# FoX attention with its decay as a table in memory, MLA attention with key halves side by side and whole second values, both written as ordered lists

## Chip, cores and metric

The kernel runs on one core of a Trainium2 chip. The metric is the device time in microseconds (us) of one execution, as the median of several; lower is better. The core's engines are TensorE (PE, matrix products; PEld is its load of the stationary operand), VectorE (DVE), ScalarE (ACT), GpSimd (POOL) and SyncE (SP, which here issues all DMAs). They run side by side and wait for each other through semaphores.

## The reference, cut to what matters

Two layers on a stream of 256 positions by 1024 features, all in float32. Each layer is a half-step SwiGLU network (1024 to 2 x 2816 and back), an attention mixer, a second half-step network and a gated input embedding, with a LayerNorm after each. The two mixers are what the change touches:

```python
# layer 0: forgetting attention (FoX), 16 heads of 64
cum = cumsum(log_sigmoid(f_logit), axis=1)            # [head, position]
s = q @ k.T / 8 + cum[:, :, None] - cum[:, None, :]   # then the causal mask, softmax, @ v
# layer 1: multi-head latent attention (MLA), 16 heads; keys and values from a shared latent
s = (q_nope @ k_nope.T + q_rope @ k_rope.T) / sqrt(192)   # 128 + 64 wide; then mask, softmax
o = softmax(s) @ v                                        # v: 128 per head
```

Sequence blocks are 128 long. Block 0 of the queries sees keys 0 to 127, block 1 sees keys 0 to 255.

## The kernel before, in words

**Split products.** Nearly every product is made of float32 numbers split in two: a high part rounded to the type float32r and a low part, the remainder. ACT writes the high part and DVE the low one (`parts`, line 497; for weights `split`, line 174). `mm3` (line 482) then issues three products, high x high, high x low and low x high, which add up in one PSUM bank. All 1 MB pieces of weights come over SP into three raw buffers, are split into ten or more slots, and are used in the order of a recording made beforehand. The steps `S.fill`, `S.ahead`, `S.later`, `S.split_now` and `S.pump` decide, when the program is built, where in ACT's and DVE's queues the next weight is split: `ahead` puts the high part now and leaves the low one, `later` puts that low one, `fill n` splits until n weights are ready beyond the one in use.

**FoX** (`fox`, line 858). After the values, a chain of small operations (`gates`, line 938, pieces s1 to s6, taken one at a time between weights) makes the running sum of the gates in a tile of 32 x 256 on ACT, DVE and POOL, and writes -8 x the sum, split in two, into `negc`. Heads go in pairs j = 0 to 7, one head on the PE's upper 64 rows and one on the lower 64. For a pair: keys and queries (`gen_k`, `gen_q`, 2.7 us of PE each), `QK` (line 1017), whose first products put the gates' term into the bank by a stationary column that selects one head (`sel` x `negc`, 384 columns), then `least` (line 1038; adds the causal mask and takes the least scaled value per row), `exps` (ACT), `divide` (reciprocals on DVE, four divisions on POOL), `T` (transposes of the probabilities on PE, then `parts`), `AV` (line 1097). `O` multiplies by the output weights. A loop over pairs of pairs (line 1146) sets the order.

**MLA** (`mla`, line 1272). The order of all steps is a list of strings, `ORDER` (line 47), that a loop at line 1556 carries out. For each head h: `gen` (keys and queries without position), `QK` (line 1449), `sm` (softmax: two DVE minima with the mask, two exponentials), `div`, `T`, `AV` (line 1512) and `O`. A query block's scores are three products of the split halves and two with the rotary keys, each 128 columns wide for block 0 and 256 for block 1. `AV` has, for the first 128 keys, three products of 256 columns, and for the second 128 keys, which only block 1 sees, three products of 128 columns with values split in two (`V` at line 1307 writes the high part, `vlo` at line 1319 the low one).

Of the kernel before, what the change touches and what calls it, by code (L numbers as in the profile page):

```python
# [45 lines left out]
VRING = ((0, 0), (1, 1), (1, 2), (2, 2))  # L46
ORDER = (
# [43 lines left out]
class Recorder:  # L91
# [10 lines left out]
    lend = reclaim = check = load = busy = pair = split = split_pieces = ahead = later = split_now = fill = pump  # L102
# [3 lines left out]
class Stream:  # L106
# [173 lines left out]
    def pair(self, n):  # L280

        self.busy(act=n)
        self.dve_t = max(self.dve_t, self.act_t + 100)
        self.busy(dve=n)
# [113 lines left out]
class Trunk:  # L398
    def __init__(self, nc, pools, a, S, rec):
        self.nc, self.a, self.S = nc, a, S  # L400
        self.sb, self.ps = pools
        self.rec = rec
        self.bg = deque()
        self.setup()
# [92 lines left out]
    def parts(self, hi, lo, src):  # L497

        self.nc.scalar.activation(hi, src, AF.Copy)  # L499
        self.nc.vector.tensor_tensor(lo, src, hi.bitcast(F32), op=ALU.subtract)  # L500
        self.S.pair(cols(src))
# [356 lines left out]
    def fox(self, li):  # L858
# [60 lines left out]
        sel = self.tl([128, 16], F32R, "sel", 1)  # L919
        negc = self.tl([128, 384], F32R, "negc", 1)  # L920
# [6 lines left out]
        nc.gpsimd.memset(negc.bitcast(F32), 0.0)  # L927
        sf = fs[:, 1792:1808]
        nc.gpsimd.tensor_tensor(sf, self.ident[:, 16:32], self.ident[:, 48:64], op=ALU.add)
        nc.gpsimd.tensor_tensor(sf, sf, self.ident[:, 80:96], op=ALU.add)  # L930
        nc.gpsimd.tensor_tensor(sel, sf, self.ident[:, 112:128], op=ALU.add)
# [4 lines left out]
        m8 = fs[fr, 1536:1792]  # L936

        def gates():
# [4 lines left out]
            def s1():  # L943
# [3 lines left out]
                self.S.busy(act=2400)  # L947
# [19 lines left out]
            def s4():  # L967
                nc.scalar.activation(negc[fr, 0:128], m8[:, 0:128], AF.Copy)
                nc.scalar.activation(negc[fr, 128:384], m8, AF.Copy)
# [127 lines left out]
        def AV(j, what=None):  # L1097
# [11 lines left out]
            if what:  # L1109
                what()  # L1110
# [35 lines left out]
        for a in range(0, 6, 2):  # L1146
# [6 lines left out]
            if a:  # L1153
                AV(a - 1)
# [519 lines left out]
```

## Time and profile before

| | |
|---|---|
| median of 3 runs | 1069.97 us (1069.09 to 1071.38) |
| the profiled execution's own time | 1069.07 us |
| its span, first to last instruction | 1067.3 us |
| mean granted TensorE clock | 0.998 |
| FoX attention, first QK to the last output product | from about 224 to 302 us of the span |
| MLA attention, first key generation to the last output product | from about 729 to 855 us |

The profile is one execution on the chip. Engine records of PE overlap, because products are pipelined; a distance from start to start is the pace. A page gives busy time and share of each engine, the chain of work that ended last, groups of instructions by line, and DMA issues. The trace behind it answers by window, by tile, by group and as a timeline. An arrow `a<-b,c` reads "a is written from b and c". Names as `h`, `y`, `tr` are PSUM banks, `P` probabilities, `PT` their transposes, `g` values or gates, `fs` the gates' scratch tile (in MLA the latent and rotary keys), `negc` the gates' term.

### The profile page before, as it was taken

The page shows a single profiled execution, that of the slowest core. Times are in us where ns is not written, and L with a number is a line of the kernel's source. Part 1 is how long each engine was busy: PE and PEld are TensorE (multiplying, and loading weights), DVE is VectorE, ACT ScalarE, POOL GpSimd, SP SyncE. Part 2 cuts the span into 40 slices and gives each one's busy share as a digit, 9 for nine tenths or more (in the row PEclk, how much of TensorE's full clock was granted, in tenths as well). Part 3 has the DMA queues.
Part 4 walks back from the last instruction along what each step waited for, and adds up shares of the span by engine and source line. Part 5 has one row for each costly group of instructions (what it writes and reads, how often), then busy time and mean ns, then how long its engine had stood idle before and what let it go on. Part 6 is the DMA issues. An engine that isn't in the chain of part 4 may idle for free.

```text
span 1067.3 us, 17503 instructions
## 1 busy us (share of the span) xinstructions
PE 1056.7 (99%) x7236; PEld 970.6 (91%) x7236; DVE 718.1 (67%) x1029; ACT 542.6 (51%) x805; POOL 68.1 (6%) x94
## 2 busy tenths in 40 slices
PE   9999999999999999999999999999999999999996
PEld 8989998999889999998899998989999889898986
DVE  6675555878797545458966464578887886454566
ACT  5564442667645434444565454436675466354431
POOL 0000000233200000000330000000000000000000
PEclk9999999999999999999999999999999999999999
DMA  8885643543348655454487555413434568555502
GB/s 299 325 295 215 247 162 119 186 175 121 115 180 301 232 186 192 146 203 139 169 294 259 180 194 187 154 59 123 137 140 158 198 244 308 181 204 182 191 4 79
DMA packets 33091, 199.58 MB, mean 187 GB/s; under 512 B 3698, under 2 KB 5490, under 8 KB 12148
## 3 DMA queue, kind: packets, MB, share of 16 engines
q1 hardware_dynamic: 33012, 198.47, 51.8%
q8 instruction: 57, 0.93, 0.4%
q14 instruction: 22, 0.18, 0.1%
HBM read 197.40 MB, written 1.05 MB: 186 GB/s over the span
## 4 chain that ended last, share of the span: by engine, by line
PE 97%; issue 1%; POOL 0%; DVE 0%; ACT 0%; DMA 0%; SPq 0%; DVEq 0%; ACTq 0%; POOLq 0%
PE y L490 36%; PE h L490 35%; PE tr L490 23%; PE tr L494 2%; DMA raw<-in_w_dram 0%; PE h L494 0%; PE tr L1087 0%; DVE x L575 0%; POOL fs L957 0%; POOL fs L950 0%; ACT hl L194 0%; SPq L360 0%; SPq L476 0%; POOL fs L956 0%; ACT hl L232 0%
## 5 line engine op out<-in xcount | busy, mean ns | idle before, releaser
L195 DVE TENSOR_TENSOR hl<-raw,hl 128x1024 fp32r<-128x1024 f32 (+2 forms) x260 | 305.7, 1194 | 146.7 <-ACT hl L194 146.1
L194 ACT ACTIVATE hl<-raw 128x1024 fp32r<-128x1024 f32 (+2 forms) x260 | 262.9, 1031 | 183.4 <-PE y L490 97.5
L490 PE MATMUL h<-xT,hl 128*128 128x256 f32 x1584 | 187.8, 278 | 1.1 <-DVE hl L234 0.5
L490 PEld LDWEIGHTS h<-xT,hl 128*128 128x128 f32 x1584 | 184.3, 189 | 2.5 <-ACT xT L499 0.9
L490 PE MATMUL y<-hl,g 128*128 128x512 f32 x792 | 185.6, 390 | 0.0
L490 PEld LDWEIGHTS y<-hl,g 128*128 128x128 f32 x792 | 147.5, 188 | 29.8
L490 PE MATMUL tr<-xT,hl 128*128 128x256 f32 x1464 | 170.8, 277 | 0.0
L490 PEld LDWEIGHTS tr<-xT,hl 128*128 128x128 f32 x1464 | 168.6, 188 | 0.5
L490 PE MATMUL h<-hl,xT 128*128 128x512 f32 (+2 forms) x294 | 65.2, 373 | 0.0
L490 PEld LDWEIGHTS h<-hl,xT 128*128 128x128 f32 x294 | 51.9, 188 | 9.7 <-DVE xT L500 0.3
L490 PE MATMUL y<-hl,xT 128*128 128x512 f32 (+3 forms) x330 | 59.7, 331 | 0.0
L490 PEld LDWEIGHTS y<-hl,xT 128*128 128x128 f32 x330 | 50.1, 188 | 5.6 <-ACT xT L499 0.4
L567 POOL TENSOR_TENSOR rs<-ve,mhalf 128x1 f32<-128x1 f32 x16 | 15.1, 943 | 619.3 <-DVE ve L566 619.3
L500 DVE TENSOR_TENSOR g<-P,g 128x512 fp32r<-128x512 f32 x38 | 26.3, 693 | 26.6 <-ACT g L499 26.6
L490 PE MATMUL y<-hl,otb 128*128 128x512 f32 x168 | 42.9, 396 | 0.0
L499 ACT ACTIVATE xT<-tr 128x512 fp32r<-128x512 f32 x28 | 16.2, 597 | 48.8 <-PE tr L494 48.8
L499 ACT ACTIVATE g<-P 128x512 fp32r<-128x512 f32 x38 | 24.0, 632 | 32.7 <-DVE P L684 32.7
L195 DVE TENSOR_TENSOR qk<-raw,qk 128x1024 fp32r<-128x1024 f32 (+2 forms) x23 | 28.0, 1217 | 16.1 <-ACT qk L194 16.1
L195 DVE TENSOR_TENSOR otb<-raw,otb 128x1024 fp32r<-128x1024 f32 (+1 forms) x22 | 26.5, 1206 | 17.7 <-ACT otb L194 17.7
L490 PEld LDWEIGHTS y<-hl,otb 128*128 128x128 f32 x168 | 30.2, 188 | 5.6
L194 ACT ACTIVATE otb<-raw 128x1024 fp32r<-128x1024 f32 (+1 forms) x22 | 22.9, 1039 | 19.4 <-PE y L490 10.8
L194 ACT ACTIVATE qk<-raw 128x1024 fp32r<-128x1024 f32 (+2 forms) x23 | 24.0, 1045 | 16.3 <-PE tr L490 6.6
(264 smaller groups left out, 1431.9 us busy)
## 6 DMA issues: line engine op xcount, KB each, us to landing
raw<-in_ffn_in_dram SPq DMA_DIRECT2D x85, 1024.0 KB, 5.0
raw<-in_ffn_out_dram SPq DMA_DIRECT2D x44, 1024.0 KB, 5.0
raw<-in_pg_dram SPq DMA_DIRECT2D x8, 1024.0 KB, 4.8
raw<-in_mo_dram SPq DMA_DIRECT2D x8, 1024.0 KB, 4.7
raw<-in_kq_dram SPq DMA_DIRECT2D x8, 640.0 KB, 4.1
gb<-in_ln_g_dram SPq DMA_DIRECT2D x8, 512.0 KB, 5.8
gb<-in_ln_b_dram SPq DMA_DIRECT2D x8, 512.0 KB, 7.7
raw<-in_fk_dram SPq DMA_DIRECT2D x4, 1024.0 KB, 4.8
```

Source lines behind the costliest of these rows:

```text
L194: nc.scalar.activation(hi, src, AF.Copy)
L195: nc.vector.tensor_tensor(lo, src, hi.bitcast(F32), op=ALU.subtract)
L490: self.nc.tensor.matmul(out, lhsT, rhs, start=start, stop=stop)
L494: self.nc.tensor.transpose(out, in_, self.ident)
L499: self.nc.scalar.activation(hi, src, AF.Copy)
L500: self.nc.vector.tensor_tensor(lo, src, hi.bitcast(F32), op=ALU.subtract)
L567: nc.gpsimd.tensor_tensor(rs, ve, self.mhalf, op=ALU.pow)
```

## The change

1. **FoX, the gates' term.** The products with `sel` and `negc` are gone, and so are these tiles. The running sum times -8 is stored to DRAM (`fox_c`). For each pair j a table `mb[:, j % 2]` of 128 x 2 x 384 is loaded from there, the same row in all 128 partitions (step `dl j`, two DMAs of 128 and 256 columns per head), and POOL writes the causal mask into it (step `dm j`, two selects). `least` adds this table where it added the mask. The table lies in the space of the LayerNorm's `gb`, which is loaded after the last `least` now (step `gb`). Four steps of the gates' chain go from POOL to DVE, and its pieces come closer together.
2. **MLA, QK.** For query block 0 the products that share a stationary operand are one: the high and low key halves lie side by side as 256 columns, so that five products of 128 columns become 256, 128 and 256. The low sum stands in columns 128 to 255, and DVE adds it to the mask before the minima.
3. **MLA, second values.** The values of the second 128 keys are no longer split: they are kept as whole float32, the transposed probabilities for them as well (`tr`, an ACT copy of 128 columns), and one product replaces three. Four of the `vlo` steps go, and `T` splits 256 columns in place of 384.
4. **Lists.** FoX follows a list `FOX` as MLA follows `ORDER`, and both have finer steps: a split is a high step on ACT and a low step on DVE (`ka kd`, `qa qd`, `ta td`, `ua ud`, `oa od`, `ga gd`), the softmax is `mi` or `le`, `ex`, `rec`, `div`. Both are in a new order. In MLA the divisions of heads 2, 3, 4, 10 and 12 go from DVE to ACT.

```diff
+FOX = (
+    "gk 0", "ka 0", "kd 0", "gq 0", "qa 0", "qd 0", "gk 1", "ka 1", "kd 1", "gq 1", "qa 1", "qd 1", "hold 1",
+    "flush", "gt", "lend 0", "QK 0", "QK 1", "le 0", "ex 0", "a", "dl 2", "gk 2", "le 1", "ka 2", "kd 2",
+    "dl 3", "rec 0", "l", "ex 1", "div 0", "gq 2", "qa 2", "qd 2", "rec 1", "dm 2", "dm 3", "a", "l", "a", "l",
+    "gk 3", "ka 3", "kd 3", "T 0", "ta 0", "td 0", "ua 0", "ud 0", "div 1", "a", "l", "a", "l", "f 3", "f 4",
+    "gq 3", "qa 3", "qd 3", "AV 0", "oa 0", "T 1", "od 0", "ta 1", "td 1", "ua 1", "back", "ud 1", "QK 2",
+    "QK 3", "le 2", "AV 1", "a", "dl 4", "oa 1", "od 1", "ex 2", "le 3", "gk 4", "ka 4", "dl 5", "ex 3",
+    "rec 2", "div 2", "kd 4", "l", "gq 4", "qa 4", "qd 4", "rec 3", "div 3", "dm 5", "a", "dm 4", "l", "a", "l",
...
+    "ua 5", "f 3", "ta 5", "QK 7", "td 5", "ud 5", "f 2", "le 6", "AV 5", "oa 5", "ex 6", "f 1", "le 7", "od 5",
+    "ex 7", "lend 1", "rec 6", "div 6", "rec 7", "div 7", "gb", "O 0 0", "f 2", "O 1 0", "a", "l", "f 3",
+    "O 3 0", "O 4 0", "T 6", "ta 6", "O 2 0", "O 5 0", "td 6", "ua 6", "ud 6", "a", "l", "f 1", "f 3", "AV 6",
...
+        mb = self.tl([128, 2, 2, 384], F32, "gb", 1)
...
+        def decay_load(j):
+
+            if not self.rec:
+                o = mb[:, j % 2]
+                for c0, n in ((0, 128), (128, 256)):
+                    row = self.fox_c[2 * j, 0:1]
+                    src = bass.AP(tensor=row.tensor, offset=row.offset, ap=[[0, 128], [256, 2], [1, n]])
+                    nc.sync.dma_start(o[:, :, c0 : c0 + n], src)
+
+        def decay_mask(j):
+
+            for c0 in (0, 256):
+                o = mb[:, j % 2, :, c0 : c0 + 128]
+                nc.gpsimd.affine_select(
+                    out=o, in_=o, pattern=[[0, 2], [-1, 128]], compare_op=ALU.is_ge, fill=NEG,
+                    base=0, channel_multiplier=1,
+                )
...
             def s5():
...
+                self.dma(self.fox_c, m8[16:32, :])
+                for j in range(2):
+                    decay_load(j)
+                    decay_mask(j)
...
-            self.bg.extend((s1, rest, rest, s2, rest, rest, s3, rest, s4, s5, s6))
+            self.bg.extend((s1, s2, s3, s4, rest, rest, s5))
...
-            for s in range(2):
-                h = 2 * j + s
-                self.mm(
-                    sb[s][:, 0:384], sel[half[s], h : h + 1].to_broadcast([64, 128]), negc[half[s], :],
-                    True, False,
-                )
...
-                        out=sb[s][:, c0:c1], in0=sb[s][:, c0:c1], in1=self.mask[:, c0:c1],
+                        out=sb[s][:, c0:c1], in0=sb[s][:, c0:c1], in1=mb[:, j % 2, s, c0:c1],
...
-            o = v[t, g] = self.tl([128, 2, 512], F32R, "g4", 5)
-            nc.scalar.activation(o[:, 0, :], ps, AF.Copy)
+            if t:
+                o = v[t, g] = self.tl([128, 512], F32, "g4", 5)
+                nc.scalar.activation(o, vps.pop((g, t)), AF.Copy)
...
-            for q0, c0, c1 in ((0, 0, 128), (128, 128, 384)):
-                w = c1 - c0
-                self.mm3(
-                    b[:, c0:c1], lambda i: o[:, i, q0 : q0 + 128],
-                    lambda i: o[:, i, 256 : 256 + w], True, False,
-                )
-                for i in (0, 1 + (h % 2 if h < 8 else 1)):
-                    self.mm(b[:, c0:c1], zT[:, h, q0 : q0 + 128], kr[:, i, 0:w], False, i > 0)
+            r = 1 + (h % 2 if h < 8 else 1)
+            two = b[:, 0:256].rearrange("p (i c) -> p i c", i=2)
+            self.mm(two, o[:, 0, 0:128], o[:, :, 256:384], True, False)
+            self.mm(b[:, 0:128], o[:, 1, 0:128], o[:, 0, 256:384], False, False)
+            self.mm(two, zT[:, h, 0:128], kr[:, 0 : r + 1 : r, 0:128], False, True)
+            self.mm3(
+                b[:, 256:512], lambda i: o[:, i, 128:256], lambda i: o[:, i, 256:512], True, False)
+            for i in (0, r):
+                self.mm(b[:, 256:512], zT[:, h, 128:256], kr[:, i, :], False, i > 0)
...
+            t = P[:, 384:512]
+            nc.vector.tensor_tensor(t, b[:, 128:256], self.mask[:, 0:128], op=ALU.add)
+            seg = ((0, b[:, 0:128], t), (128, b[:, 256:512], self.mask[:, 128:384]))
...
-            self.parts(o[:, 0, :], o[:, 1, :], b[:, 0:384])
-            PT[h] = o
+            raw = self.tl([128, 128], F32, "p1", 1)
+            left["T", h] = o[:, 0, 0:256], o[:, 1, 0:256], b[:, 0:256]
+            left["raw", h] = raw, b[:, 256:384]
+            PT[h] = o, raw
...
-            for m, (i, jj) in enumerate(((0, 0), (0, 1), (1, 0))):
-                self.mm(
-                    ps[:, 128:256], v[1, g][:, i, c : c + 128], o[:, jj, 256:384], False, m == 2
-                )
+            self.mm(ps[:, 128:256], v[1, g][:, c : c + 128], raw, False, True)
```

More of the change, by code (lines that the diff above doesn't have):

```diff
@@ L100, in pump @@
         pass
-    lend = reclaim = check = load = busy = pair = split = split_pieces = ahead = later = split_now = fill = pump
+    lend = reclaim = check = load = busy = pair = follow = split = split_pieces = ahead = later = split_now = fill = pump
     between, hl, hold = {}, {}, False
@@ L282, in pair, with follow @@
         self.busy(act=n)
+        self.follow(n)
+    def follow(self, n):
         self.dve_t = max(self.dve_t, self.act_t + 100)
@@ L497, in parts, with high, low @@
     def parts(self, hi, lo, src):
+        self.high(hi, src)
+        self.low(hi, lo, src)
+    def high(self, hi, src):
         self.nc.scalar.activation(hi, src, AF.Copy)
+        self.S.busy(act=cols(src))
+    def low(self, hi, lo, src):
         self.nc.vector.tensor_tensor(lo, src, hi.bitcast(F32), op=ALU.subtract)
-        self.S.pair(cols(src))
+        self.S.follow(cols(src))
     def transposed(self, t, src, halves=(0, 1), ring="tr"):
@@ L918, in fox @@
         bf = self.tl([128, 1], F32, "bf", 1)
-        sel = self.tl([128, 16], F32R, "sel", 1)
-        negc = self.tl([128, 384], F32R, "negc", 1)
+        self.tl([128, 16], F32, "gap2", 1)
+        mb = self.tl([128, 2, 2, 384], F32, "gb", 1)
         cq = self.tl([128, 16, 2], F32, "cq", 1)
@@ L999, in fox, with high, g, low @@
         VA(1)
-        st, PT = {}, {}
+        st, PT, left = {}, {}, {}
         qk = self.own([128, 2, 2, 512], F32R, "qk")
+        def high(f):
+            def g(j):
+                for hi, _, src in left[f, j] if isinstance(left[f, j], list) else [left[f, j]]:
+                    self.high(hi, src)
+            return g
+        def low(f):
+            def g(j):
+                x = left.pop((f, j))
+                for y in x if isinstance(x, list) else [x]:
+                    self.low(*y)
+            return g
         OT = []
@@ L1008, in gen @@
             o = qk[:, j % 2]
-            self.parts(o[:, 0, c0 : c0 + 256], o[:, 1, c0 : c0 + 256], ps[:, 0:256])
+            left[key, j] = o[:, 0, c0 : c0 + 256], o[:, 1, c0 : c0 + 256], ps[:, 0:256]
         def gen_k(j):
@@ L1425, in zT_last, with high, g, low @@
             S.busy(act=512)
-        st, PT = {}, {}
+        st, PT, left = {}, {}, {}
+        def high(f):
+            def g(h):
+                hi, _, src = left[f, h]
+                self.high(hi, src)
+            return g
+        def low(f):
+            return lambda h: self.low(*left.pop((f, h)))
+        def raw_copy(h):
+            self.high(*left.pop(("raw", h)))
         def gen(h):
@@ L1446, in gen @@
             o = home["qk"][:, h % 2]
-            self.parts(o[:, 0, :], o[:, 1, :], ps)
+            left["gen", h] = o[:, 0, :], o[:, 1, :], ps
         def QK(h):
@@ L1550, in mla @@
             dq=dq, rms=rms, dqs=dq_scale, cqT=cq_transpose, V=V, vlo=vlo, qr=q_rope, rope=rope, rc=rope_copy, rot=rotate, zT=zT_first,
-            zs=z_split, zU=zT_last, gen=gen, QK=QK, sm=softmax, div=divide, T=T, AV=AV, O=O, y=room, hold=hold,
+            zs=z_split, zU=zT_last, gen=gen, QK=QK, mi=minima, ex=exps, rec=recip, div=divide, T=T, AV=AV,
+            ga=high("gen"), gd=low("gen"), ta=high("T"), tr=raw_copy, td=low("T"), oa=high("AV"), od=low("AV"), O=O, y=room, hold=hold,
             f=S.fill, a=S.ahead, l=S.later, XT=lambda t, n: self.XT(t, (n,)),
```

176 lines of the change are left out of this document (57 added, 119 removed), and 69 rows, old and new, of tables (FOX, ORDER).

## The prediction, made before the changed kernel ran

> **What bounds the kernel now.** I read the page first, then the chain of waits, the busy times by window, and the timeline of the two attention stages. A row has its start and its length in us, then engine, line, operation, out<-in, shape and count.
>
> ```profile
> span 1067.3 us, 17503 instructions
> ...
> PE 1056.7 (99%) x7236; PEld 970.6 (91%) x7236; DVE 718.1 (67%) x1029; ACT 542.6 (51%) x805; POOL 68.1 (6%) x94
> ...
> PE 97%; issue 1%; POOL 0%; DVE 0%; ACT 0%; DMA 0%; SPq 0%; DVEq 0%; ACTq 0%; POOLq 0%
> ```
>
> TensorE (PE) is busy for 99% of the span and is 97% of the chain that ended last. Records overlap in the pipeline, so a duration there is no price; prices are the distances from start to start. A piece of the chain gives one, and the windows (length, then busy us of PE, PEld, DVE, ACT, POOL, granted clock, DMA share, GB/s) give the room beside it:
>
> ```profile
> 28.35 10.88 PE h L490 x96
> ```
> ```profile
> 224.00:242.00 18.00, 18.00 (x174) 17.36 (x174) 14.14 (x41) 11.15 (x31) 6.05 (x8) 1.00 0.57 212
> 735.00:760.00 25.00, 25.00 (x179) 23.15 (x179) 21.58 (x53) 16.11 (x39) 0.00 (x0) 1.00 0.30 98
> ```
>
> A 256-column product costs 10.88/96 = 113 ns. In both stages that change PE never idles at full clock, and VectorE (DVE), the next one, is 79% (14.14/18) and 86% (21.58/25) busy. So PE work that goes is worth its price, as long as nothing else comes late.
>
> **MLA, on PE.** One head's AV, then the next head's QK, then key generation:
>
> ```profile
> 745.83 0.80 PE L490 MATMUL h<-PT,g 128*128 128x256 f32 x6
> 746.47 0.50 PE L490 MATMUL tr<-qk 128*128 128x128 f32 x3
> 746.80 0.39 PE L490 MATMUL tr<-fs,xT 128*128 128x128 f32 x2
> 747.03 0.57 PE L490 MATMUL tr<-qk 128*128 128x256 f32 x3
> 747.44 0.40 PE L490 MATMUL tr<-fs,xT 128*128 128x256 f32 x2
> 747.67 0.85 PE L490 MATMUL h<-fs,hl 128*128 128x256 f32 x6
> ```
>
> QK takes 747.67 - 746.47 = 1.20 us: five 128-column products in 0.56 (112 ns each, as much as 256 columns cost) and five 256-column ones in 0.64. Side by side, the five narrow ones become 256, 128 and 256. Eight products are then 8 x 113 = 0.90 to 8 x 128 = 1.02 us (0.64/5 = 128 holds the extra 0.07 at the change of width). That saves 0.18 to 0.30; I take 0.28, nearest to the 113 row, since only one change of width is left.
>
> AV takes 0.64: three 256-column products (0.34) and three 128-column ones (0.30). These three become one product of whole fp32 values. The trace has one such product, the 384-column warm-up:
>
> ```profile
> 2.00 0.85 PE L466 MATMUL y<-mask 128*128 128x384 f32 x1
> 2.65 1.06 PE L494 MATMUL tr<-ident 128*128 128x128 f32 x4
> ```
> ```profile
> 750.76 0.49 PE L494 MATMUL tr<-ident,P 128*128 128x128 f32 x3
> ```
>
> One call leaves two records; this is the second, 0.65 us to the next start, so 0.217 per 128 columns. PE is then at about half pace: four transposes take 1.06, while later three take 0.49 (some 0.6 for four). Warm, a pass should cost 0.108 and the product, two passes, 0.217. AV saves 0.30 - 0.217 = 0.08, at most 3 x 0.112 - 0.217 = 0.12; at the early pace it loses 0.30 - 0.433 = -0.13. I take 0.09. Per head 0.37, in 16 heads **5.9 us** (0.05 to 0.42 per head: 0.8 to 6.7).
>
> **FoX, on PE.** The third QK block, two pairs of heads on 64-row halves that run together:
>
> ```profile
> 239.03 0.38 PE L494 MATMUL tr<-ident,P 128*128 128x128 f32 x2
> 239.34 0.44 PE L490 MATMUL y<-negc,sel 64*128 64x384 f32 x2
> 239.62 0.86 PE L490 MATMUL y<-qk 64*128 64x128 f32 x12
> 240.31 0.33 PE L490 MATMUL y<-negc,sel 64*128 64x384 f32 x2
> 240.48 0.85 PE L490 MATMUL y<-qk 64*128 64x128 f32 x12
> 241.26 0.97 PE L490 MATMUL h<-PT,g 128*128 128x512 f32 x3
> ```
>
> The gate products (negc) cost 240.48 - 240.31 = 0.17 inside a block and 0.28 at its entry, where 0.11 is start-up that the first qk pair may inherit. All go: 4 x (0.17 + 0.17) = **1.4 us** in four blocks, 0.9 if the entry's goes over to the next pair nearly whole, 1.8 if nothing does.
>
> **Beside PE, MLA.** Group rows (count | busy us, mean ns):
>
> ```profile
> L500 DVE TENSOR_TENSOR PT<-tr,PT 128x384 fp32r<-128x384 f32 x16 | 8.8, 549 | 0.7 <-ACT PT L499 0.7
> L500 DVE TENSOR_TENSOR otb<-h,otb 128x256 fp32r<-128x256 f32 x10 | 4.2, 416 | 0.5 <-ACT otb L499 0.5
> L1470 DVE CUSTOM_DVE_ANT_0 tr<-tr,mask 128x128 f32<-128x128 f32 x16 | 4.7, 292 | 0.0
> ```
>
> DVE gains 16 adds of 128 columns (some 0.29 each, 4.7 us) and loses 16 x (0.549 - 0.416) = 2.1 in the remainders of P and four value remainders of 512 columns, at least 0.55 each, 2.2: nothing on balance, since five divisions leave it as well. ScalarE (ACT), 64% busy (16.11/25), takes these five and 16 short copies of whole P. PE's products hide all of it, so I cost it at nothing; where a head's chain outlasts that cover, it is rival A. **The order**: PE's list in MLA is the old one but for seven swaps of neighbours, and in FoX but for the output products, so no product is moved to a place where its operands are much younger, with one exception below; what moves is where ACT and DVE do their pieces. That costs nothing by itself and can lose or win only at waits, of which the windows show none.
>
> **Beside PE, FoX.** The table's way is new: POOL writes m8, a store, broadcast loads, POOL masks, then the minima.
>
> ```profile
> 217.64 0.41 POOL L964 TENSOR_SCALAR fs<-fs 32x256 f32<-32x256 f32 x1 [1.08 <-DVE fs L963]
> ```
> ```profile
> 225.09 0.30 DVE L1044 CUSTOM_DVE_ANT_0 y<-y,mask 128x128 f32<-128x128 f32 x1 [0.33 <-PE y L490]
> ```
> ```profile
> out_dram<-x SPq DMA_DIRECT2D x3, 256.0 KB, 2.0
> g<-in_p_dram SPq DMA_DIRECT2D x4, 128.0 KB, 4.9
> gb<-in_ln_b_dram SPq DMA_DIRECT2D x8, 512.0 KB, 7.7
> ```
> ```profile
> L455 POOL TENSOR_SCALAR_AFFINE_SELECT mask<-mask 128x128 f32<-128x128 f32 x2 | 0.5, 295 | 1.2 <-PE y L466 1.2
> ```
>
> m8 ended at 218.05; four POOL steps go to DVE, so I take 216. Store 2.0, loads 0.8 to issue and 4.9 to land, two selects of 256 columns 0.6 to 1.2 (one to two times 295 ns each): 224.3 to 224.9, just before the minima's 225.09. With no gain, and store and loads at 7.7 each: 218.05 + 15.4 + 1.2 = 234.7, 9.6 late. I take 0 and keep that end. T 0 gives 0.8 of it back (next rows). Two waits are added on SP, for m8 and for the store to land, and each later load waits for the minima two pairs before; behind them on SP stand weight loads alone, which have three raw buffers and ten split slots ahead, so that is free. In all 16 loads of 3.1 MB (8 x 128 x 768 x 4 bytes) join a DMA share of 0.57. On DVE four steps of some 0.41 (L964's shape) come in and three conversions go; weight splits queue behind them, under the same ten slots.
>
> ```profile
> 230.92 2.43 POOL L1076 TENSOR_SCALAR P<-P,su 128x128 f32<-128x128 f32 x4 [12.88 <-DVE su L1072]
> ```
> ```profile
> 234.15 0.60 PE L1087 MATMUL tr<-ident,P 128*128 128x128 f32 x4
> ```
> ```profile
> 228.94 0.16 DVE L1051 TENSOR_TENSOR tt<-tt,cq 128x4 f32<-128x4 f32 x1
> ```
> ```profile
> 232.87 4.11 POOL L1076 TENSOR_SCALAR P<-P,su 128x256 f32<-128x256 f32 x5
> 238.59 0.60 PE L1087 MATMUL tr<-ident,P 128*128 128x128 f32 x4
> ```
>
> T 0 follows its divisions (end 233.35) by 0.8, T 1 (ends 236.98) by 1.6. The new list puts masks 2 and 3 ahead of division 1 on POOL, and mask 3 waits for loads that follow minima 1 (229.1): + 0.4 + 4.9 = 234.4, its selects to 235.6, four divisions of 2.43 to 3.6 us (232.87 + 4.11 - 233.35) to 238.0 to 239.2, against T 1 at about 238.2. Bounds 0 and, with a landing of 7.7, 3.8; I take **0.6 us lost**. Later tables load a pair ahead of their use and mask after the divisions. The exception is T 6: one output product less stands before it.
>
> ```profile
> 280.25 1.63 POOL L1076 TENSOR_SCALAR P<-P,su 128x128 f32<-128x128 f32 x4 [10.22 <-DVE su L1072]
> ```
> ```profile
> 282.87 0.60 PE L1087 MATMUL tr<-ident,P 128*128 128x128 f32 x4
> ```
> ```profile
> 297.76 0.74 DVE L575 SCALAR_TENSOR_TENSOR x<-x,mv,gb 128x512 f32<-128x512 f32 x1
> ```
>
> Its divisions end at 281.88, 1.0 ahead. Six products of 512 columns less (12 x 113 = 1.36) and the block's 0.34 less bring T 6 to 281.2; the list puts minima 7 ahead of AV 5's remainders on DVE, so that the divisions end between 280.5 and 282.3: 0 to 1.1 lost, I take 0. The LayerNorm's gb now loads after minima 7, which end before 280.25: + 0.8 + 7.7 = 288.8, well before 297.76: free.
>
> **Sum.** 5.9 + 1.4 - 0.6 = 6.7 us. The profiled execution took 1069.07 (span 1067.3 and 1.8 around it): 1062.4. The median of the runs shown, 1069.97, is 0.9 above it, so I forecast **1063.3**.
>
> **Rivals.** (A) MLA is bound by a head's chain, not by PE. QK to T gets 0.29 longer, T to AV 0.13 shorter, and PE gives 0.37 less cover. For: DVE is 86% busy. Against: the window shows no PE idle time, and other products lie between. All lost: 1063.3 + 5.9 = 1069.2; half: 1066.2. (B) The whole-value product costs four 128-column slots: 4 x 0.112 = 0.45 against 0.30 (the early pace gives 0.433), so AV loses 0.13 instead of gaining 0.09: 16 x 0.22 = 3.5, 1066.8. For: fp32 has no warm row. Against: the warm-up left two records, not four. The Trainium skill, "FP8 and Floating Point Precision", section "TensorE Precision Notes", speaks against the change: true FP32 takes four passes through the array, where the split takes three. By it, at this kernel's price of a narrow product, the time is B's; the trace agrees only as far as the two records each run at two columns' time per column. (C) Slower: the table's store and loads queue behind weight loads. Place: T 0; price 9.6 - 0.8 = 8.8, so 1063.3 + 8.8 = 1072.1; it turns the gain into a loss once minima 0 starts after about 233. For: 212 GB/s in that window, and one late landing holds everything behind it on SP. Against: a DMA share of 0.57, and three landings in a row at the worst row. (D) Stalls go with the finer order or the bounds fall low: under 1060.7.
>
> **How the numbers follow.** Forecast 0.62 (1060.7 to 1065.5), A 0.17, B 0.08, C 0.07, D 0.06. The low end is the sum with 6.7, 1.8, no lost 0.6 (1061.5) and 0.8 for stalls removed; the high end, 1067.5, takes in B and half of A. A measurement of this kernel tells 0.2% from no change (1067.8 and 1072.1). Faster: 0.62 + 0.06 + 0.08 + 0.11 of A = 0.87; same: 0.06 of A + 0.02 of C = 0.08; slower 0.05.
>
> **What would show it.** MLA QK from 1.20 to about 0.92 and AV from 0.64 to 0.55, start to start; two fp32 records of about 108 ns per AV (B: over 200); no negc rows, FoX blocks of 1.92 at about 1.58. PE idle before T (A) or before T 0 and T 1 (C, the lost 0.6). I am wrong if PE's idle time in the two stages grows by more than 2 us.

## The result, and the profile after

The changed kernel takes **1067.79 us** (median of 14 runs, 1065.49 to 1068.79), the kernel before, run beside it, 1070.15 (14 runs, 1068.83 to 1072.72): a ratio of 0.9975, 95% interval 0.9966 to 0.9983. It is faster by 2.4 us where 6.7 were forecast, and lies just above the range given (1060.7 to 1067.5).

Two profiles are compared by the starts of products that both kernels have. The **FoX stretch** runs from the first QK product of FoX to the first output product of the FFN behind it, the **MLA stretch** from key generation 0 to the first output product of the last FFN. "Changed, again" is a later run of the same kernel (e14). A "remainder" below is the low half that DVE writes from a PSUM bank; the bank is free for the next product when it is done. Numbers behind T, QK, AV and "division" are those of the pair in FoX and of the head in MLA.

| stretch (us) | before | changed | changed, again |
|---|---|---|---|
| start to first output product of FFN 1 | 60.83 | 63.43 | 61.02 |
| that FFN, up to its last output product | 126.96 | 126.94 | 126.96 |
| from there to FoX's first QK | 36.14 | 35.54 | 35.92 |
| FoX | 134.66 | 135.85 | 135.91 |
| FFN, per-layer embedding, FFN, MLA's start | 370.03 | 370.03 | 370.04 |
| MLA | 174.17 | 170.62 | 170.72 |
| last FFN and end | 164.50 | 164.58 | 164.58 |
| span | 1067.3 | 1067.0 | 1065.2 |

MLA gains 3.55 (5.9 forecast), FoX loses 1.19 (a gain of 0.8 forecast), the stretch ahead of it gains 0.2 to 0.6. The first stage, 2.6 longer in the first pair of profiles, is no part of the change (run e14). The busy times on the page of the changed kernel:

```profile
span 1067.0 us, 17478 instructions
...
PE 1053.0 (99%) x7172; PEld 965.5 (90%) x7172; DVE 716.0 (67%) x1032; ACT 545.7 (51%) x829; POOL 69.5 (7%) x100
```

The windows of the two stretches in the kernel before and then in the changed one (length, then busy us of PE, PEld, DVE, ACT, POOL, granted clock, DMA share, GB/s):

```profile
223.93:358.59 134.66, 134.62 (x997) 123.80 (x997) 106.77 (x211) 81.94 (x168) 24.36 (x34) 1.00 0.52 190
...
728.62:902.79 174.17, 174.13 (x1196) 159.66 (x1195) 143.71 (x277) 107.04 (x204) 1.84 (x2) 1.00 0.51 183
```
```profile
225.91:361.75 135.84, 134.23 (x981) 122.33 (x981) 108.58 (x213) 83.42 (x170) 33.02 (x48) 1.00 0.61 214
...
731.78:902.40 170.62, 169.71 (x1148) 154.60 (x1147) 141.81 (x280) 111.54 (x230) 1.85 (x2) 1.00 0.53 187
```

PE was never idle in either stretch before (0.04 us each); now it is idle for 135.84 - 134.23 = 1.61 us in FoX and for 0.91 in MLA. In FoX POOL is busy for 33.0 us, no longer 24.4. POOL, DVE and PE where T 1 stands (timelines of the changed kernel, start and length in us; in brackets the idle time just before and what ended it):

```profile
235.25 3.45 POOL L989 TENSOR_SCALAR_AFFINE_SELECT gb<-gb 128x256 f32<-128x256 f32 x4
...
238.68 3.65 POOL L1137 TENSOR_SCALAR P<-P,su 128x128 f32<-128x128 f32 x4
...
238.90 2.36 DVE L239 TENSOR_TENSOR hl<-raw,hl 128x1024 fp32r<-128x1024 f32 x2
...
240.21 0.27 PE L1148 MATMUL tr<-ident,P 128*128 128x128 f32 x1
241.58 1.13 PE L1148 MATMUL tr<-ident,P 128*128 128x128 f32 x3 [1.10 <-POOL P L1137]
...
242.55 0.38 PE L530 MATMUL tr<-ident,P 128*128 128x128 f32 x2
...
242.86 1.65 PE L526 MATMUL y<-qk 64*128 64x128 f32 x24
...
244.44 0.73 PE L526 MATMUL h<-PT,g 128*128 128x512 f32 x2
```

The QK block takes 244.44 - 242.86 = 1.58, as forecast, but T 1's second transpose comes 1.27 us behind its turn, and the two behind it 0.24 and 0.35: **1.85 us** for a term of 0.6. (The first, at 240.21, is in time; a turn is 0.109 us after the one before.) The four selects of masks 2 and 3 took 3.45 us of POOL, where I had 1.2 to 2.4, and division 1 another 3.65.

MLA in the changed kernel: AV and QK of two middle heads, then AV 0.

```profile
757.28 0.52 PE L526 MATMUL h<-PT,g 128*128 128x256 f32 x3
757.64 0.38 PE L526 MATMUL h<-p,g 128*128 128x128 f32 x2
757.78 0.95 PE L526 MATMUL h<-fs,hl 128*128 128x256 f32 x6
...
761.35 0.34 PE L526 MATMUL tr<-qk 128*128 128x256 f32 x2
761.52 0.33 PE L526 MATMUL tr<-fs,xT 128*128 128x256 f32 x1
761.69 0.52 PE L526 MATMUL tr<-qk 128*128 128x256 f32 x3
762.05 0.39 PE L526 MATMUL tr<-fs,xT 128*128 128x256 f32 x2
762.27 1.55 PE L526 MATMUL y<-hl,otb 128*128 128x512 f32 x6
```
```profile
745.15 0.68 DVE L543 TENSOR_TENSOR qk<-h,qk 128x512 fp32r<-128x512 f32 x1
...
745.55 0.33 ACT L539 ACTIVATE p<-tr 128x128 f32<-128x128 f32 x1
...
745.97 0.59 PE L526 MATMUL h<-PT,g 128*128 128x256 f32 x3 [0.76 <-ACT p L539]
```

QK takes 762.27 - 761.35 = 0.92 in this head, as forecast; of the fourteen QK of single heads in the trace nine take 1.02 or more (see below). AV takes 757.78 - 757.28 = 0.50 to the next start; that product starts 0.03 us behind the last record of AV and the one after it 0.20 later, so AV itself is nearer 0.58, for 0.55 forecast. PE is idle for 0.76 us before AV 0's first product, which starts 0.92 us behind its turn. The profile names the copy of the whole weights p (ACT, end 745.88), which AV 0's last product reads; the bank of all of them, which key remainder 2 frees (DVE, end 745.83), comes at nearly the same time.

### The profile page after: what moved, and what is told of

The parts are those of the page before. It is cut to its first block, busy times and chain, and to the rows that moved or that the text cites. A ratio compares the mean times of both kernels' runs of the same rounds, so it can differ in the third digit from the quotient of the medians.

```text
span 1067.0 us, 17478 instructions
## 1 busy us (share of the span) xinstructions
PE 1053.0 (99%) x7172; PEld 965.5 (90%) x7172; DVE 716.0 (67%) x1032; ACT 545.7 (51%) x829; POOL 69.5 (7%) x100
## 4 chain that ended last, share of the span: by engine, by line
PE 75%; DVE 1%; ACT 1%; POOL 1%; issue 1%; DVEq 0%; POOLq 0%
PE y L526 29%; PE h L526 26%; PE tr L526 18%; PE tr L530 2%; POOL P L1137 0%; PE h L530 0%; PE tr L1148 0%; POOL gb L989 0%; DVE x L618 0%; DVE qk L543 0%; ACT P L1122 0%; DVE hl L228 0%; ACT qk L539 0%; ACT P L1504 0%; DVE hl L239 0%
## 5 line engine op out<-in xcount | busy, mean ns | idle before, releaser
L228 DVE TENSOR_TENSOR hl<-raw,hl 128x1024 fp32r<-128x1024 f32 (+3 forms) x258 | 302.8, 1193 | 139.4 <-ACT hl L227 138.8
L227 ACT ACTIVATE hl<-raw 128x1024 fp32r<-128x1024 f32 (+3 forms) x258 | 260.3, 1031 | 173.4 <-PE y L526 93.6
L239 DVE TENSOR_TENSOR hl<-raw,hl 128x1024 fp32r<-128x1024 f32 (+2 forms) x28 | 33.1, 1194 | 2.2 <-ACT hl L235 2.2
L726 ACT ACTIVATE P<-tr 128x512 f32<-128x512 f32 x20 | 12.0, 600 | 42.6 <-PE tr L526 42.6
```

The source lines that it names most:

```text
L726: nc.scalar.activation(gt, ps[0], AF.Silu)
```

## Experiments

Theory: the changes of PE's products are priced about right, and what is missing went into new waits, T 1 in FoX (POOL between two divisions), AV 0 and a few others in MLA. Rivals: the new order of steps is the real gain or the real loss; the whole-value product costs more than its two records; the missing time is the first stage, which is 2.6 us longer. All stretches below are read as above, each from one profiled execution; the two of the changed kernel agree within 0.1 us in both stretches. A wait of PE is given as the time that a start lies behind its turn, which is some 0.16 us more than the idle time in brackets (0.92 for 0.76 at AV 0).

### e1: masks behind division 1

```diff
-"rec 1", "dm 2", "dm 3", "a", "l",        +"rec 1", "a", "l",
-"ud 0", "div 1", "a", "l",                +"ud 0", "div 1", "dm 2", "dm 3", "a", "l",
```

> The changed kernel with one edit: masks 2 and 3 stand behind division 1 on POOL, not ahead of it. Theory (T 1's 1.85 us are the four mask selects, 235.25 to 238.70, that POOL does between divisions 0 and 1): division 1 starts as division 0 ends, at about 235.3, T 1's stalls go to 0.1 or less, and the stretch from the first FoX QK product to the first output product of the next FFN goes from 135.85 to about 134.0 us. Minima 2, which now stand 0.1 to 0.2 behind the masks, may take up to 0.5 of it. Rival 1 (mask 3's loads landed late and held POOL): the selects wait wherever they stand and division 1, now ahead of them, no longer does, so T 1's stall goes as well, but POOL then shows an idle wait of over 1 us ahead of mask 3. Rival 2 (T 1 waits for PE's own order or for a bank, not for POOL): the stretch stays within 0.2 of 135.85.

Measured: FoX 134.64, T 1 without a stall; in the next run, with the same FoX lists, 134.39. The divisions and selects there (timeline of e2):

```profile
230.42 6.08 POOL L1137 TENSOR_SCALAR P<-P,su 128x128 f32<-128x128 f32 x8 [6.13 <-DVE su L1130]
236.46 3.45 POOL L989 TENSOR_SCALAR_AFFINE_SELECT gb<-gb 128x256 f32<-128x256 f32 x4
```

POOL goes from division to division, and the selects follow without a wait for a landing: rival 1 falls. In the changed kernel, too, the selects start as division 0 ends (235.25). 0.46 us come back at AV 1, whose second product waited for T 1's remainder. The masks cost FoX 1.2 to 1.5 us.

### e2: the whole copy early

The lists of e1, and `"T 0", "ta 0", "tr 0", "td 0", ...` where `"tr 0"` had stood five steps further.

> The edit of the kernel with late masks, and a second one: the whole copy of head 0's weights for token tile 1 stands on ACT right behind the rounding copy of the same head, ahead of a weight split, a key copy and what follows. Theory (the whole-value way put a copy on the path, and at AV 0 it queues behind a weight split of 1.1 us): the stall of 0.92 us before AV 0's last product goes to 0.2 or less, and the stretch from key generation 0 to the first output product of the last FFN goes from 170.62 to about 169.8 us. Rival (AV 0 waits for the remainders on DVE or for another late operand as well): 170.3 to 170.6, with a new stall at AV 0 or T 1.

Measured: 170.80. My theory fell: AV 0 still waits.

```profile
740.33 0.69 DVE L1328 TENSOR_TENSOR g<-y,g 128x512 fp32r<-128x512 f32 x1
...
740.72 0.33 ACT L539 ACTIVATE p<-tr 128x128 f32<-128x128 f32 x1
...
741.08 0.42 DVE L543 TENSOR_TENSOR PT<-tr,PT 128x256 fp32r<-128x256 f32 x1
...
741.42 0.68 DVE L543 TENSOR_TENSOR qk<-h,qk 128x512 fp32r<-128x512 f32 x1
...
742.25 0.59 PE L526 MATMUL h<-PT,g 128*128 128x256 f32 x3 [0.85 <-DVE qk L543]
```

The whole weights are there at 741.05; now the bank alone is late. Key remainder 2 stands on DVE behind a value remainder (0.69), which the new list had moved ahead of AV 0, and behind T 0's. The profile names the last of several late operands only.

### e3, e9: side-by-side QK alone, with and without its add

e3 is the kernel before with the new QK products and minima in the old order. e9 leaves the add out:

```diff
-            t = P[:, 384:512]
-            nc.vector.tensor_tensor(t, b[:, 128:256], self.mask[:, 0:128], op=ALU.add)
-            seg = ((0, b[:, 0:128], t), ...
+            seg = ((0, b[:, 0:128], self.mask[:, 0:128]), ...
```

> The kernel before with one part of the change alone: the products of MLA's QK side by side, and the one more add that the minima then need; softmax, order and everything else as before. The trace of the changed kernel says that QK's price fell by 19.28 - 15.85 = 3.4 us in 16 heads. If that is its price by itself and the add is hidden, the stretch from key generation 0 to the first output product of the last FFN goes from 174.17 to 170.7 (my prediction's 0.28 a head: to 169.7). Rival (the add of 128 columns lengthens the head's chain, which DVE ends late in the old order, where a softmax is one step): 171.5 to 174, with new stalls before T.

> The kernel before with side-by-side QK products and nothing else, as in the run with QK alone, but without the added add: the second half of the double product (the scores' low-order part for the first token tile) is left out of the minima and of the softmax. With the add, the stretch from key generation 0 to the first output product of the last FFN took 176.71, 3.3 us of products less than before and 5.8 us more of other time. Theory (the add of 0.29 us on DVE lies in each head's chain and makes T, AV and the banks late): the waits go and the stretch is 170.9 to 171.5. Rival (not the add, but the cover: QK to T has 0.2 us less of PE work beside it): 174 or more.

Measured: 176.71 with the add, 172.90 without. Alone and in the old order, an edit that makes PE's products 3.3 us shorter makes MLA **2.5 us longer**. The windows of e3 and e9:

```profile
732.00:908.70 176.70, 174.21 (x1164) 156.45 (x1163) 148.01 (x293) 105.88 (x204) 1.84 (x2) 1.00 0.50 181
```
```profile
729.63:902.53 172.90, 172.26 (x1164) 156.54 (x1163) 143.58 (x277) 106.25 (x204) 1.84 (x2) 1.00 0.51 184
```

DVE is busy for 4.4 us more with the add (148.01 against 143.58), and PE's idle time goes from 0.64 to 2.49. One such place in e3: AV 2's second product waits for T 2's remainder, which DVE does after a key remainder.

```profile
757.00 0.68 DVE L500 TENSOR_TENSOR qk<-h,qk 128x512 fp32r<-128x512 f32 x1
...
757.60 0.55 DVE L500 TENSOR_TENSOR PT<-tr,PT 128x384 fp32r<-128x384 f32 x1
...
758.20 0.79 PE L490 MATMUL h<-PT,g 128*128 128x256 f32 x5 [0.54 <-DVE PT L500]
```

So the add accounts for 3.8 us here, more than e3's rival allowed. The 2.0 left (172.90 against 170.9) were not taken apart: e9 lies between its theory and its rival, and 0.64 us of them show as idle time of PE. That they come of the thinner cover is argued, not shown.

### e4, e6, e7, e8_order_values: each edit in each order

e4 is the kernel before with whole second values alone. The other three are the changed kernel with split values and the narrow QK (e6), with split values only (e7), with the narrow QK only (e8_order_values). "New order" takes in the five divisions on ACT. In e6 and e7 the four value remainders that the new list lacks stand right behind their high halves, a place that nobody tuned, so that part of what whole values are worth there may be that place.

> The kernel before with the other part alone: the second token tile's values and weights whole, one fp32 product in place of three narrow ones; the copy of the whole weights stands right behind the pair that splits the others. The trace of the changed kernel says 0.07 a head: the stretch from key generation 0 to the first output product of the last FFN goes from 174.17 to about 173.1 (my prediction's 0.09: 172.7). If four slots of a narrow product were the price after all (a loss of 0.13 a head): 176.2. If the copy on ACT comes late by 0.1 or more a head: 173.5 to 175, with idle time of PE before the fp32 product.

> The changed kernel with both product edits of MLA taken back (narrow QK products one by one, the minima without the added add, second values and weights split, three narrow products in AV), but with the new order of finer steps. Theory (the gain is the products', 3.4 for QK and 1.1 for AV, and the new order alone only adds its stall of about 1 us at AV 0): the stretch from key generation 0 to the first output product of the last FFN is 174.2 + 1.0 = about 175.1. Rival (the new order is the gain): 172.5 or less.

> The changed kernel with split second values (three narrow products in AV, as before), but with side-by-side QK in the new order. Theory (QK is worth 3.4 in the new order, the whole values 1.1): 170.62 + 1.1 = 171.7 for the stretch from key generation 0 to the first output product of the last FFN, where the old order with the same QK took 176.71. Rival (whole values matter more than their price, since they relieve DVE): 173 or more. Other rival (they cost as much as they save): 170.4 to 170.9.

> The changed kernel with the narrow QK products and their minima as before, but with whole second values and the new order. In the new order the stretch from key generation 0 to the first output product of the last FFN took 174.78 with neither edit, 173.42 with side-by-side QK, 170.62 with both. If the edits add up (the values are worth 2.8 us wherever they stand): 174.78 - 2.80 = 172.0. Theory (the values' own price on PE is 1.7 at most; the rest of the 2.8 is DVE time that they give back to the heads' chain that the add of QK had lengthened): 173.0 to 174.3.

Measured, the MLA stretch in us:

| | old order | new order |
|---|---|---|
| neither edit | 174.17 | 174.78 |
| side-by-side QK | 176.71 | 173.42 |
| whole values | 176.14 | 172.70 |
| both (the change) | not run | 170.62 |

The new order by itself loses 0.6. It is what makes the edits pay: in it QK is worth 1.4 us (2.1 beside whole values), whole values 2.1 (2.8 beside the new QK); in the old order both lose. e4's loss is waits of 0.85 us before an output product, 0.57 at AV 2 and 1.09 in the last FFN's first products; that its 176.14 is the figure for four slots (176.2) is chance, as e5 shows.

To separate price from waits, every product in the stretch is put at the steady price of its shape (256 columns 115 ns, 128 columns 109, 512 columns 227), and the rest is "beyond". In the kernel before, where PE never waits, that rest is 174.17 - 171.85 = 2.32.

| new order | products | beyond |
|---|---|---|
| neither | 171.85 | 2.93 |
| QK | 168.56 | 4.86 |
| values | 170.11 | 2.60 |
| both | 166.81 | 3.81 |

QK's products are 3.29 shorter, 0.205 a head and not 0.28, and 1.9 of it (1.2 beside whole values) come back beyond them; the idle time of PE grows by 1.1 (0.36 to 1.48) and 0.8 (0.11 to 0.91). The values' products are 1.74 shorter and bring 0.3 more (1.1 beside the new QK). My theory for e7 (171.7) fell; its first rival holds. e6 (174.78) is near its theory, e8_order_values (172.70) lies between the sum of the edits and my theory.

### e5: the whole-value product twice

> The changed kernel with the whole-value product of each head issued twice, so that the second token tile's part counts twice in the output. The stretch from key generation 0 to the first output product of the last FFN is 170.62 in the changed kernel. Theory (the product is two passes of 108 ns, as its records say): 16 x 0.217 = 3.5 us more, 174.1. Rival of the prediction (it costs four slots of a narrow product, 0.45): 7.2 more, 177.8. If PE has slack there that hides it: less than 3 more.

Measured: 173.85, 3.23 more or 0.20 us a product. That is near two passes of 108 ns (3.5); four narrow slots would have been 7.2.

### e11: the masks ahead, two weight splits moved

```diff
-"div 1", "a", "l", "a", "l", "f 3", "f 4",     +"div 1", "f 3", "f 4",
-"back", "ud 1",                                +"back", "ud 1", "a", "l", "a", "l",
```

> The changed kernel with masks 2 and 3 still ahead of division 1 on POOL, but with the two weight splits on DVE that ran beside division 1 (238.90 to 241.26) moved behind T 1's remainders. In the changed kernel one division of 256 columns beside them took 2.50 us where its neighbours took 0.48, and two of the four selects, beside two earlier splits, 1.38 and 1.39 where the others took 0.40. Theory (POOL stands still while DVE works on two operands from SBUF): the four divisions take 1.7 us in place of 3.65 and T 1's stall goes from 1.85 to 0.3 or less, with the masks where they are; minima 2 may then come late by up to 2.4 us behind the splits. Rival (a division's length has nothing to do with DVE, only the selects cost): the divisions stay at 3.65 and T 1 waits 1.5 us or more.

```profile
230.37 2.43 POOL L1137 TENSOR_SCALAR P<-P,su 128x128 f32<-128x128 f32 x4 [6.11 <-DVE su L1130]
232.76 3.44 POOL L989 TENSOR_SCALAR_AFFINE_SELECT gb<-gb 128x256 f32<-128x256 f32 x4
236.19 1.62 POOL L1137 TENSOR_SCALAR P<-P,su 128x128 f32<-128x128 f32 x4
```

Division 1 takes 1.62 in place of 3.65, and T 1 does not wait, with the masks where the change had put them. So the stall needs both: selects ahead of division 1, and splits on DVE beside division 1. The stretch itself is 136.34, since a later query product started 1.80 us late: its bank waited for AV 1's remainders (245.21 to 246.06), which DVE did behind the moved splits and minima 2.

### e8_repaired, e10, e13: the waits taken away in the lists

e8_repaired is e2 with AV 0's remainders behind T 1's (FoX), key remainder 2 ahead of T 0's and of the value remainder, T 10's remainder ahead of minima 11, and `"rec 12", "div 12 0", "l", "a",` for `"rec 12", "l", "a", "div 12 1",`. e10 moves that value remainder and two splits behind T 1's remainder, e13 the value remainder alone.

> The kernel with late masks and the early whole copy, with four more moves in the lists: in FoX, AV 0's remainders stand behind T 1's on DVE (AV 1 waited 0.46 us for T 1's); in MLA, key remainder 2 stands ahead of T 0's and of a value remainder of 0.69 us (AV 0 waited 1.0 us for its bank until key remainder 2 was done), T 10's remainder ahead of minima 11 (AV 10 waited 0.37), division 12 on DVE right behind its reciprocals (T 12 waited 0.40). Theory (each of these waits goes and nothing else comes late): the FoX stretch goes from 134.39 to about 133.9, the MLA stretch from 170.80 to about 169.4, and the time to about 1063.2, against 1065.0 with late masks and the early copy, and 1067.8 for the changed kernel. Rival (each moved step only hands its wait to the next): the two stretches stay within 0.4 of 134.4 and 170.8, and the time at 1064.5 or more.

> The repaired kernel with one more move in MLA: the value remainder (0.68 us) and two weight splits (1.2 us on DVE) that stood ahead of key remainder 3 and of T 1's remainder stand behind them. Theory (AV 1 waited 0.59 + 0.13 us for its bank, which key remainder 3 gives free, and AV 0's stall had only been handed on): the MLA stretch goes from 170.63 to about 169.9, the FoX stretch stays, and the time is about 1064.5. Rival (the splits only move the wait on again, to AV 2 or to output product 0): 170.5 or more and 1065.2.

> The repaired kernel with one more move in MLA: the value remainder of 0.68 us stands behind T 1's remainder and no longer ahead of key remainder 3; the splits stay where they are, unlike in the second repair, where output product 0 waited 1.76 us. Theory (AV 1's 0.59 + 0.13 us are this remainder's 0.68): the MLA stretch goes from 170.63 to about 170.1. Rival (its bank is wanted by the first output product, which then waits): 170.5 or more.

| | time, median (runs) | ratio to before, interval | FoX | MLA |
|---|---|---|---|---|
| e8_repaired | 1065.22 (5) | 0.9960, 0.9945 to 0.9975 | 134.73 | 170.63 |
| e10 | 1066.88 (7) | 0.9970, 0.9958 to 0.9982 | 134.81 | 172.01 |
| e13 | 1065.48 (9) | 0.9961, 0.9947 to 0.9975 | 134.42 | 170.62 |
| changed, beside e13 | 1067.66 (12) | 0.9981, 0.9969 to 0.9994 | 135.91 | 170.72 |

With these lists the kernel is 2.2 us faster than the change beside it on the same chip (1065.48 against 1067.66), and 1.5 of it is FoX; the intervals to before still overlap. In MLA the rivals' figures came each time. In e8_repaired AV 0's wait fell from 1.01 to 0.25 and AV 1 got one of 0.59, as key remainder 3 was now the late one. In e10 the splits that were moved left output product 0 waiting for 1.76. In e13 only the figure is the rival's: output product 0 does not wait, and AV 1 is still 0.45 late.

### e12: the changed kernel without the add

The edit of e9 in the changed kernel.

> The changed kernel without the add that side-by-side QK needs in the minima: the second half of the double product is left out of the scores of the first token tile. In the old order the add alone made the stretch from key generation 0 to the first output product of the last FFN 3.8 us longer (176.71 with it, 172.90 without). Theory (in the new order the add still lies in the heads' chains and is what makes head 10 to 12 late; AV 0's wait has another cause, a value remainder and a key remainder on DVE): 170.62 less 0.3 to 0.8, with AV 0's wait of 0.9 still there. Rival 1 (the add is what stands between 3.3 us of saved products and the 1.4 to 2.1 that came of them): 169.4 or less. Rival 2 (the new order hides the add): within 0.2 of 170.62.

Measured: 169.84, 0.8 less. In the new order the add costs 0.8 us, not 3.8. AV 0's wait is 0.63 there, against 0.92 with the add. The other runs in the new order have it as 0.52 with neither edit (e6) and as 0.28 with whole values and the narrow QK (e8_order_values): part of it is the order's, the rest comes with the new QK, of which the add is 0.3.

### e14: the changed kernel again

> The changed kernel itself, on the chip of the two others, for a comparison of times with the repaired one and for the length of its first stage. Theory (the 2.6 us by which the first FFN product of the changed kernel's profile came late, 63.43 against 60.83, belong to the run and not to the change): the first stage is near 61 us when a block of 96 products takes 10.88 there, near 63 when it takes 11.31, and the stages behind it repeat within 0.2: FoX 135.85, MLA 170.62. Rival (it belongs to the changed program): 63.4 again, whatever its blocks take.

The first stage took 61.02, and the stretches behind it repeat to 0.1, but for 0.38 ahead of FoX. Products of 256 columns, 96 to a chunk, in the changed kernel and then in its second run (start of each chunk; a length takes in the last product's overlap):

```profile
18.20 11.47 PE L526 MATMUL tr<-xT,hl 128*128 128x256 f32 x96
29.51 5.82 PE L526 MATMUL h<-xT,hl 128*128 128x256 f32 x48
```
```profile
17.50 11.04 PE L526 MATMUL tr<-xT,hl 128*128 128x256 f32 x96
28.38 5.60 PE L526 MATMUL h<-xT,hl 128*128 128x256 f32 x48
```

From start to start 96 products take 29.51 - 18.20 = 11.31 us in the one and 28.38 - 17.50 = 10.88 in the other: 118 or 113 ns each, in the same program. e3 and e13 show 11.31 in their chains too, e8_repaired 10.88.

## Why the prediction was wrong

The direction was right; the size was not, and the median fell just outside the range. The step that failed is the one that put the work of DVE, ACT and POOL at nothing or little: MLA has 1.5 us more beyond its products, 0.9 of it idle time of PE, where 0 was taken, and T 1 lost 1.85 for 0.6. A price came on top, QK's 0.28 a head for 0.205. By its own steps (the two profiles of the changed kernel give the ranges at the end):

| step | forecast | measured |
|---|---|---|
| MLA, QK | -4.5 | -1.4 to -2.1 (products -3.3) |
| MLA, AV | -1.4 | -2.1 to -2.8 (products -1.7) |
| MLA, order | 0 | +0.6 |
| MLA in all | -5.9 | -3.55 (products -5.0) |
| FoX, four QK blocks | -1.4 | -1.2 |
| FoX, T 1 | +0.6 | +1.85 |
| FoX, the rest | 0 | +0.5 |
| ahead of FoX | 0 | -0.2 to -0.6 |
| last FFN and end | 0 | +0.1 |
| sum | -6.7 | -2.3 to -2.9; median -2.4 |

**"I take 0.28, nearest to the 113 row".** The 1.20 before was one row of an untypical head, and the 0.92 came true only where QK follows other products than transposes. Another view of the kernel before: with transposes ahead of it QK takes 757.85 - 756.62 = 1.23,

```profile
756.62 0.53 PE L490 MATMUL tr<-qk 128*128 128x128 f32 x3
756.99 0.39 PE L490 MATMUL tr<-fs,xT 128*128 128x128 f32 x2
757.21 0.56 PE L490 MATMUL tr<-qk 128*128 128x256 f32 x3
757.62 0.40 PE L490 MATMUL tr<-fs,xT 128*128 128x256 f32 x2
757.85 2.95 PE L490 MATMUL y<-hl,otb 128*128 128x512 f32 x12
```

and in the changed kernel, after transposes, 1.02 (head 5: 773.99 to 775.01); behind other products the two take 1.15 and 0.93. Like against like the saving is 0.21 a head, inside the 0.18 to 0.30 that I had worked out: 1.2 us of the miss.

**"PE's products hide all of it, so I cost it at nothing".** This step failed, for the side of DVE and ACT. PE idle at zero means only that nothing was late by more than the cover; it gives no measure of the slack. The added add is 4.4 us of DVE work in the heads' chains. In the old order it costs 3.8 us, in the new one 0.8 (e3, e9, e12). The largest other part is AV 0, 0.92 late, whose bank came late (in e2, with its operands there, it is as late). I had named this as rival A. Of the 2.35 us that MLA lost, 0.9 are prices (products -5.04 for -5.9) and 1.5 came beyond the products (2.32 to 3.81), so rival A came about by a quarter at most, not by the half that I had priced.

**"... so no product is moved to a place where its operands are much younger".** This failed at AV 0. Its own place is the old one, but the value remainder had moved ahead of key remainder 2 on DVE; with the order alone AV 0 is 0.52 late (e6), and in the kernel before it is in time. The order on the engine that frees a bank counts as much as PE's.

**AV.** Right in its mechanism and too small: 2.1 to 2.8 us for 1.4. Rival B is refuted by e5. The four passes of the Trainium skill, "FP8 and Floating Point Precision", section "TensorE Precision Notes", do not show as four slots: the product costs 0.20 us, as two narrow ones do.

**T 1.** The wait was foreseen, and sized at 0.6 for 1.85. The sum began with mask 3's loads landing at 234.4, and that did not bind: the selects start as division 0 ends. Two things were left out. A select takes 0.40 us by itself but 1.38 beside a weight split; and the divisions behind it slow down in the same way. One view of each group of the changed kernel (shortest, median and longest in ns):

```profile
L989 POOL TENSOR_SCALAR_AFFINE_SELECT gb<-gb x16: 403/408/1391, 222.1 to 275.0; 128x256 f32<-128x256 f32 x16
```
```profile
L1137 POOL TENSOR_SCALAR P<-P,su x4: 370/428/2496, 238.7 to 241.9; 128x128 f32<-128x128 f32 x2, 128x256 f32<-128x256 f32 x2
```

The division of 2.50 us ended 0.27 us behind the two splits beside it (241.53 and 241.26). The Trainium skill, "SBUF — State Buffer", section "Who interferes with whom", has a rule for it: a DVE instruction with two SBUF inputs contends with a GpSimd instruction that reads SBUF, and the ports that they share are an exclusive lock. A split subtracts one SBUF tile from another. e11 agrees: without the splits division 1 takes 1.62. With these durations in my own sum division 1 ends at 233.35 + 3.45 + 3.65 = 240.45, 2.2 us behind T 1's turn at 238.2, where 1.85 was measured.

**The table's way.** Rival C did not come about: minima 0 wait for PE alone, as before, and T 0 for nothing. But the table's second pair did cost, in POOL's queue and not in the landing.

**FoX, the rest.** Three QK blocks take 1.58 for 1.92, as forecast; the fourth takes 2.11 for 2.28, since its second pair of heads waits for a bank that a remainder on DVE frees:

```profile
276.24 0.22 PE L526 MATMUL h<-qk 64*128 64x128 f32 x1
276.70 0.93 PE L526 MATMUL h<-qk 64*128 64x128 f32 x11 [0.24 <-DVE otb L543]
```

The further 0.5 us is small pieces, summed from start to start by kind of product: 0.2 in the output products, 0.2 in transposes of P (0.14 at T 6, where I took 0), 0.1 in AV and the LayerNorm's transposes. The key and query products add nothing: one row of 72 takes 8.48 us where it took 8.18, and another 8.17 where it took 8.48. In the second run of the changed kernel T 1 loses 1.6, and these products take 0.4 more, to nearly the same sum.

What stays open: why the output products take 0.2 more, what the rest beyond the products is made of where PE shows no idle time, and what the gain ahead of FoX comes from.

## What to carry to other kernels

An engine that is never idle says that the others are in time, not by how much: before shortening its work, work out for each operand and each bank the time between its last writer and its turn, and do not take from that what the edit adds to the other engines. A price that is a difference must be taken from two places with the same neighbours. And on POOL, do not take an operation's duration from a row where it ran alone: here it ended with its neighbour on DVE where that one read two tiles of SBUF (1.39 us for 0.40, 2.50 for 0.48).

## What the runs showed of the hardware

- The same stream of 256-column products ran at 113 or at 118 ns each for a whole stage in two runs of one program, at a granted clock of 1.00. From the chunks shown to the first output product that is 45.23 us against 43.52; the first FFN takes 126.96, or 128.13 to 128.16 in e1, e3, e9, e8_order_values and e13. Such a difference is of the size of what was to be measured, so stretches of two profiles were compared and not spans.
- POOL's select of 256 columns takes 0.40 us or 1.39, its division of 256 columns 0.48 or 2.50, beside two-tile splits on DVE (0.40 and 0.48 beside remainders, which read one operand from PSUM).
- A product of whole fp32 values with 128 columns takes 0.20 us, as much as two narrow products of split halves (e5).
